# The opening of a pooling-mixer kernel: rows of both halves loaded first, stores queued behind the third product's operand, root steps on GpSimd

## The chip, the cores and the metric

The kernel runs on one core of one Trainium2 chip. Its time is the device time of one execution in microseconds (us); a kernel's time is the median over its runs. A profiled execution has its own time, and a span: from the first to the last instruction that the profiler recorded. The engines are TensorE (PE in the profile, its weight loads PEld), VectorE (DVE), ScalarE (ACT), GpSimd (POOL) and SyncE (SP), which here only issues DMAs.

## The reference

```python
def rms_norm(x, w):
    y = xf * lax.rsqrt(jnp.mean(xf * xf, axis=-1, keepdims=True) + RMS_EPS)
    return y * w

def pool_mixer(h, in_w, group_w, group_b, scale, out_w):
    u, gate = jnp.split(h @ in_w, 2, axis=-1)
    ug = u.reshape(b, s, POOL_GROUPS, POOL_GROUP_DIM)         # 4 groups of 256
    pooled = jnp.stack([trailing_mean(ug[:, :, g], w)         # windows 2, 4, 8, 16
                        for g, w in enumerate(POOL_WINDOWS)], axis=2) - ug
    mixed = jnp.einsum('bsgc,gcd->bsgd', pooled, group_w) + group_b
    y = mixed.reshape(b, s, POOL_WIDTH) * scale * jax.nn.silu(gate)
    return y @ out_w

def reference(x, norm_w, ...):                                # DEPTH = 1: mixer 0 alone
    h = x + pool_mixer(rms_norm(x, norm_w[0]), ...)
    return rms_norm(h, final_norm_w)
```

x is 1 x 4096 x 1024 (4096 rows of 1024), all in float32; in_w is 1024 x 2048, out_w 1024 x 1024, group_w four 256 x 256 matrices.

## The kernel before, in words

**Products.** Every big product is cut into 2 x 2 blocks and done by seven block products instead of eight (P1 to P7, a scheme of Strassen's kind): the operands are sums and differences of blocks, formed on VectorE, and PSUM banks gather the results. Each float32 operand is split into a high part, a copy by ScalarE (L151, `copy`), and a low part, a subtract by VectorE (L145, `sub`). `mm3` (L512) then takes three matmuls for each pair: high x high, high x low, low x high. A block product of the input side is 48 matmuls of 128 x 128 by 128 x 512: 2 halves of the depth, 4 banks, 2 parts, 3 each.

**Steps.** A list of 112 steps is written out by hand: 28 "a" steps (4 blocks of 1024 rows x seven products; the first 512 columns of gate and value), 28 "b" steps (the second 512), 56 "o" steps (8 blocks of 512 rows, out_w). Inside a block the order is `ORDER_IN = (P1, P2, P6, P7, P5, P4, P3)`, so P6 is the third product and P5 the fifth. A loop goes through the steps: it loads operands some steps ahead, forms and splits those of the next ones, runs the product's matmuls and evicts the banks. Before that loop the first two products (`run(0)`, `run(1)`) and the opening are written out by hand. A scheduler puts each engine's instructions in one in-order queue, by the order in the program, by `high_priority` and by `issue_after`, which keeps an instruction behind another one. An engine waits at the head of its queue; what stands behind waits too.

**The opening.** Fourteen dummy matmuls on a zeroed tile come first (L900). Then group_w is multiplied into the value half of in_w (`fold`, L334): two sides q = 0, 1 of four chunks; a chunk takes its part of the transposed in_w (`wut`, one 512 KB load), 16 records of a 128 x 256 matmul, and an eviction of two banks by ScalarE with the column `norm_c` (L346). The second side's four results are stored to memory (`wvd`, POOL's DMA queue, L955) and used by "b" steps. P1 of the first block follows.

**Row factors.** The rms norm's factor of each row is needed along the free axis, as P1's outputs stand with rows along it. `load_row` loads four 128-row groups for each half of a block (half 0 and 1; 512 KB each), `square_row` (L365) squares them on ScalarE with row sums into `ss`, and `stats` and `rsqrt` (L187 to L196) make 1/sqrt: mean (DVE, L372), Sqrt (ACT), reciprocal (L190) and one Newton step (four small DVE instructions of 128 x 4). In the first block `spread_rs` brings these columns to all partitions: `hl` is their split in two parts, two DVE multiplies (L389) with the identity `ident` write them out into `w[P7][0]`, and two matmuls with a tile of ones (L396) sum over partitions into bank 7, which ScalarE copies to `rstd`. Half 0 and half 1 each have such a spread, called between the banks of P1. Later blocks go through a small DRAM buffer `rd`.

**The third product's operand.** P6 of the first block needs the transposed x of both halves (tiles "11", "12", "21", "22"; loaded raw, `xt`). `normalize` (L411, by L148) multiplies "21" and "22" by rstd of half 1, `form` subtracts twice (`sub` to "21", then to "2"), `split_step(2)` splits "2" into two operand tiles `op`. `normalize_raw` does the multiplies of "11" and "12" by rstd of half 0 and stores the results (`sd`) for the "b" steps. P1's and P2's banks of the first block are evicted by DVE multiplies with rstd (`evict_in`). The weights of P7, P5, P4 and P3 are split on the way (L145 with w, `rest_of_first`), their memory being used before that for the opening's loads (`early`, `early5`).

**Tile names.** `st_…`, `vt_…`, `op_…`, `bank_…` with numbers in the prediction are uses of a tile in program order: st_91 and vt_101 hold "11" and "12" in part, vt_100 is a tile of "12", op_85 to op_88 are operand tiles in turn.

**The tail.** In the last output block sums of squares are made by halves: `early_half`, `late_factor` (one root for each of the last rows) and `late_half` (the multiply by the factor and the store).

Of the kernel before, what the change touches and what calls it, by code (L numbers as in the profile page):

```python
# [15 lines left out]
P = 128  # L16
# [44 lines left out]
def kernel(  # L61
# [82 lines left out]
    def sub(dst, a, b):  # L144
        nc.vector.tensor_tensor(out=dst, in0=a, in1=b, op=ALU.subtract)  # L145
# [7 lines left out]
    def split(dst, src):  # L153

        copy(dst[:, 0], src)
        sub(dst[:, 1], src, dst[:, 0].bitcast(F32))
# [30 lines left out]
    def rsqrt(dst, tmp, ms):  # L187

        nc.scalar.activation(tmp, ms, AF.Sqrt)
        nc.vector.reciprocal(out=dst, in_=tmp)  # L190
        mul(tmp, dst, ms)
        mul(tmp, tmp, dst)
        nc.vector.tensor_scalar(
            out=tmp, in0=tmp, scalar1=-0.5, scalar2=1.5, op0=ALU.mult, op1=ALU.add
        )
        mul(dst, dst, tmp)  # L196
# [123 lines left out]
    def load_wut(q, k, by=2):  # L320
        r = take("p (k t c) -> p k t c", early5, k=2, t=4)
        for kk in range(0, 2, by):
            nc.sync.dma_start(
                out=r[:, kk : kk + by],
                in_=wut[q, k + kk : k + kk + by].rearrange("k p t c -> p k t c"),
            )
        return r

    def fold(q, k, g, r, ps2, o, on_vector=False):

        for kk in range(2):
            for j in range(2):
                for t in range(2):
                    nc.tensor.matmul(  # L334
                        ps2[kk][:, j * 256 : (j + 1) * 256],
                        r[:, kk, 2 * j + t, :],
                        g[:, 2 * j + t, :],
                        start=(t == 0),
                        stop=(t == 1),
                    )  # L340
            if on_vector:
                last = nc.vector.tensor_scalar(
                    out=o[:, kk], in0=ps2[kk], scalar1=norm_c[k + kk], scalar2=None, op0=ALU.mult
                )
            else:
                last = nc.scalar.activation(o[:, kk], ps2[kk], AF.Copy, scale=norm_c[k + kk])  # L346
        give(r)
        return last
# [21 lines left out]
    def stats(b, half):  # L370
        ms = small.tile([P, 4], F32, tag="ms", name=f"ms{b}_{half}")
        nc.vector.tensor_scalar(  # L372
            out=ms, in0=sums[b, half], scalar1=1.0 / D, scalar2=EPS, op0=ALU.mult, op1=ALU.add
        )
        tmp = small.tile([P, 4], F32, tag="tmp", name=f"tmp{b}_{half}")
        rs = small.tile([P, 4], F32, tag="rs", name=f"rs{b}_{half}")
        rsqrt(rs, tmp, ms)
        return rs
# [3 lines left out]

    def spread_rs(half, rs):

        hl = small.tile([P, 2, 4], F32R, tag="hl", name=f"hl{half}")
        split(hl, rs)
# [8 lines left out]
        for s in range(2):  # L395
            nc.tensor.matmul(  # L396
                banks[7], ones, r[:, s, 0], start=s == 0, stop=s == 1, skip_group_check=True
            )
# [23 lines left out]

    def split_halves(us, saved=None, by_pool=False):
        ts = []
        for h, u in enumerate(us):
            t = next_op("p (s a b) -> p s a b", s=2, a=2)
            split(t, u)
            if saved is not None:
                (nc.gpsimd if by_pool else nc.scalar).dma_start(out=saved[h], in_=u)
# [30 lines left out]
    def form_in(q, b, i):  # L460
# [6 lines left out]
        elif i == P6:  # L467
            s["2"] = [take(pool=early if q == 0 and b == 0 else None) for _ in range(2)]
# [27 lines left out]

    def normalize_raw(i):

        for h, u in enumerate(xs[0]["11" if i == P1 else "12"]):
            normalize(0, 0, u)  # L500
            nc.gpsimd.dma_start(out=sd[0][i][h], in_=u)
# [6 lines left out]

    def mm3(ps, lt, r, start, stop):

        for n, (a, b) in enumerate(((lt[0], r[0]), (lt[0], r[1]), (lt[1], r[0]))):
            nc.tensor.matmul(  # L512
                ps, a, b, start=start and n == 0, stop=stop and n == 2, skip_group_check=True
            )
# [3 lines left out]
    def product_in(i, t, sets, by_bank, between=None):  # L518
# [4 lines left out]
        for n, (h, ct) in enumerate(halves):  # L523
# [3 lines left out]
            for kk in range(2):  # L527
                mm3(
                    ps[ct],
                    (w[i][h][:, 0, kk, c], w[i][h][:, 1, kk, c]),  # L530
                    (t[h][:, 0, kk], t[h][:, 1, kk]),
                    i in (P1, P7) and h == 0 and kk == 0,
                    h == 1 and kk == 1,
                )
# [174 lines left out]
    def mean_square(b, half, ss):  # L709
        n = ss.shape[1]  # L710
        ms = small.tile([P, n], F32, tag="ms", name=f"oms{b}_{half}")
        nc.vector.tensor_scalar(
            out=ms, in0=ss, scalar1=1.0 / D, scalar2=EPS, op0=ALU.mult, op1=ALU.add
        )
        return ms

    def inverse(b, half, ms):
        n = ms.shape[1]
        tmp = small.tile([P, n], F32, tag="tmp", name=f"otmp{b}_{half}")
        rs = small.tile([P, n], F32, tag="rs", name=f"ors{b}_{half}")  # L720
        rsqrt(rs, tmp, ms)
# [6 lines left out]
    def finish(b, half):  # L728
# [6 lines left out]
        rs = inverse(b, half, mean_square(b, half, ss))  # L735
# [18 lines left out]
    def mean_part(ss, before):  # L754

        ms = column()
        nc.vector.tensor_scalar(
            out=ms, in0=ss, scalar1=1.0 / D, scalar2=before, op0=ALU.mult, op1=ALU.add
        )
# [13 lines left out]
    def late_factor(half, j, parts):  # L773
# [6 lines left out]
        partial["last"] = nc.scalar.activation(tmp, ss, AF.Sqrt, bias=before, scale=1.0 / D)  # L780
        ms = mean_part(ss, before)
        nc.vector.reciprocal(out=rs, in_=tmp)
# [9 lines left out]
    def late_half(half, j, n, rs):  # L792
        rows = row_of(NBO - 1, half, j)
        u = hs[NBO - 1].pop((half, j))
        with tc.issue_after(partial["last"].ins):
            nc.scalar.activation(u[:, 1 - n], u[:, 1 - n], AF.Copy, scale=rs)
        nc.scalar.dma_start(out=out[rows, (1 - n) * H : (2 - n) * H], in_=u[:, 1 - n])
        nc.vector.scalar_tensor_tensor(
            out=u[:, n], in0=u[:, n], scalar=rs, in1=fw[0][:, n], op0=ALU.mult, op1=ALU.mult
        )  # L800
        nc.sync.dma_start(out=out[rows, n * H : (n + 1) * H], in_=u[:, n])

    def evict_o(b, i, sets):
# [5 lines left out]
        for j in range(2):  # L809
# [7 lines left out]
            for p in range(parts):  # L817
                c = slice(p * (H // parts), (p + 1) * (H // parts))
                add(u[:, c], ps[j][:, c], u[:, c])
                if last:  # L820
                    partial["part", p] = square_part(u[:, c])
            if last:
                factors.append(late_factor(half, j, parts))
        for j, rs in enumerate(factors):
# [43 lines left out]
    def run(n, between=None):  # L868
# [5 lines left out]
        else:  # L874
            product_in(i, split_up.pop(n), sets, i == P1, between)
# [23 lines left out]
    for c in range(14):  # L899
# [3 lines left out]
    nc.scalar.dma_start(out=colt, in_=cols)  # L903
# [5 lines left out]
    ru[0, 0] = load_wut(0, 0, by=1)  # L909
# [7 lines left out]
    for n, (h, k) in enumerate(chunks):  # L917
        if k < 4:
            o = v0[h] = take(pool=early)
        else:  # L920
            o = v1[h] = take()
        fold(0, k, gw[0], ru[0, k], banks[2 * (n % 2) : 2 * (n % 2) + 2], o)
        ru[1, k] = load_wut(1, k)
        if n == 0:
            load(0)
            g0.append(load_rows(in_w, 2, D))
            split_scaled(w[P1][0], g0[0], pair(norm_c, 0, 0))
        elif n == 1:
            split_step(0)
        elif n == 2:  # L930
            split_scaled(w[P1][1], g0[1], pair(norm_c, 1, 0))
        if n > 1:
            for j in range(2 * n - 4, 2 * n - 2):
                load_row(0, 0, j)
    give(gw[0])
    for j in range(4):
        load_row(0, 1, j, early if j < 1 else None)
    load(1)
    g1 = [load_rows(in_w, 4 + 2 * h, D) for h in range(2)]

# [11 lines left out]
    for n, (h, k) in enumerate(chunks):  # L952
        o = take(pool=early if n < 2 else early5)
        fold(1, k, gw[1], ru[1, k], banks[2 * (n % 2) : 2 * (n % 2) + 2], o)
        nc.gpsimd.dma_start(out=wvd[k // 2], in_=o)  # L955
        give(o)
        if n < 2:
            second_side(n)
            for j in range(2 * n, 2 * n + 2):
                square_row(0, 0, j)  # L960
            if n == 1:
                with tc.high_priority():
                    rs[0] = stats(0, 0)
        else:
            for j in range(2 * n - 4, 2 * n - 2):
                square_row(0, 1, j)
    give(gw[1])
    load(2)
# [7 lines left out]
    run(0, {1: lambda: spread(0), 5: lambda: spread(1)})  # L976
# [4 lines left out]
    normalize_raw(P1)  # L981
    for h in range(2):
        for key in ("21", "22"):
            normalize(0, 1, xs[0][key][h])
    form(2)
    split_step(2)
    run(1)
    normalize_raw(P2)
    give(rstd.pop(0))
    for h in range(2):  # L990
        split(w[P7][h], v0[h])
        give(v0[h])
# [58 lines left out]
    for n in range(2, len(steps)):  # L1051
# [22 lines left out]
        if n == 2:  # L1074
            form_s4(0)
            form(n + 2)
        if kind == "a" and b == 0:
            rest_of_first(n)
# [74 lines left out]
```

## Time and profile before

| | |
|---|---|
| median of 3 runs | 966.04 us (964.88 to 966.52) |
| profiled execution: time, span | 964.39 us, 962.6 us |
| mean granted PE clock | 0.997 |
| PE busy | 949.7 us, 99% |
| DVE busy | 748.4 us, 78% |
| ACT busy | 453.0 us, 47% |
| POOL busy | 6.7 us, 1% |
| DMA | 177.01 MB, mean 184 GB/s |

Busy time is the time in which an engine had an instruction under way; shares are of the span. A line of an answer names the source line, the engine, the operation, output<-input and the number of instructions. In the list of waits a line gives the waiting instruction, the engine and line it waited for, the total us, the number of waits and the us of one. In the chain of waits the first number is where a stretch begins (us from the start of the span) and the second how long it lasts. In the view by stretches each engine's column is the busy us of the stretch, with the number of instructions.

### The profile page before, as it was taken

How to read it: one execution, taken by the hardware profiler on the slowest of the kernel's cores; microseconds unless marked ns; L12 is line 12 of the kernel's file. 1: busy time of each engine (PE TensorE's matmuls, PEld its weight loads, DVE VectorE, ACT ScalarE, POOL GpSimd, SP SyncE). 2: the span in 40 equal slices, each digit the busy share in tenths (PEclk: the TensorE clock that was granted, in tenths of full speed). 3: DMA queues.
4: the chain of work that ended last, by engine and by line, in shares of the span. 5: the costliest groups of instructions: out<-in, count | busy, mean ns of one | idle time of the engine just before them, and what ended most of it. 6: DMA issues, size and time to landing. Idle time of an engine off the chain costs nothing.

```text
span 962.6 us, 11058 instructions
## 1 busy us (share of the span) xinstructions
PE 949.7 (99%) x4190; PEld 785.5 (82%) x4190; DVE 748.4 (78%) x919; ACT 453.0 (47%) x677; POOL 6.7 (1%) x16
## 2 busy tenths in 40 slices
PE   9999999999999999999999999999999999999996
PEld 8778888888888888888888888888888888888885
DVE  4699994893895997696697599499978667677675
ACT  5849447347445555345345445553423424324233
POOL 0110000000000000000000000000000000000000
PEclk9999999999999999999999999999999999999998
DMA  9965864564656646016614733645746436356022
GB/s 337 408 264 157 305 237 163 210 240 137 213 219 226 233 156 237 1 45 218 240 44 165 263 119 131 219 151 178 259 141 212 162 123 230 108 187 218 22 88 88
DMA packets 67685, 177.01 MB, mean 184 GB/s; under 512 B 6704, under 2 KB 24240, under 8 KB 67632
## 3 DMA queue, kind: packets, MB, share of 16 engines
q1 hardware_dynamic: 61728, 156.37, 46.8%
q10 hardware_dynamic: 4176, 13.65, 3.5%
q0 software_dynamic: 1728, 6.29, 1.6%
q8 instruction: 33, 0.54, 0.2%
q14 instruction: 20, 0.16, 0.1%
HBM read 116.50 MB, written 59.78 MB: 183 GB/s over the span
## 4 chain that ended last, share of the span: by engine, by line
PE 78%; DVE 13%; DMA 5%; ACT 3%; issue 1%; DVEq 0%; SPq 0%; ACTq 0%
PE bank L512 75%; PE bank L334 2%; DVE op L145 2%; DVE vt L142 2%; DMA st<-wvd 2%; DVE st L148 1%; DVE st L145 1%; DMA rd<-rs 1%; DVE st L598 1%; DVE w L145 1%; DMA st<-rd 1%; DVE st L261 1%; DVE vt L145 1%; DVE w L209 1%; DVE st L142 1%
## 5 line engine op out<-in xcount | busy, mean ns | idle before, releaser
L512 PE MATMUL bank<-op,w 128*128 128x512 f32 x2688 | 611.7, 389 | 2.5 <-ACT op L151 2.1
L512 PEld LDWEIGHTS bank<-op,w 128*128 128x128 f32 x2688 | 504.0, 188 | 109.1 <-ACT op L151 2.6
L512 PE MATMUL bank<-w,op 128*128 128x512 f32 (+1 forms) x1356 | 305.0, 387 | 0.0
L512 PEld LDWEIGHTS bank<-w,op 128*128 128x128 f32 x1356 | 253.0, 188 | 52.0
L151 ACT ACTIVATE op<-st 128x1024 fp32r<-128x1024 f32 x117 | 123.2, 1056 | 142.0 <-PE bank L512 112.2
L145 DVE TENSOR_TENSOR op<-st,op 128x1024 fp32r<-128x1024 f32 x117 | 141.5, 1217 | 38.7 <-ACT op L151 38.3
L151 ACT ACTIVATE op<-vt 128x1024 fp32r<-128x1024 f32 x49 | 51.8, 1059 | 92.2 <-PE bank L512 72.9
L142 DVE TENSOR_TENSOR vt<-vt 128x1024 f32<-128x1024 f32 (+6 forms) x72 | 87.7, 1227 | 0.1
L142 DVE TENSOR_TENSOR st<-bank,st 128x512 f32<-128x512 f32 x78 | 53.1, 686 | 36.9 <-PE bank L512 36.6
L145 DVE TENSOR_TENSOR op<-vt,op 128x1024 fp32r<-128x1024 f32 x49 | 59.8, 1220 | 21.7 <-ACT op L151 21.7
L151 ACT ACTIVATE vt<-bank 128x512 f32<-128x512 f32 x90 | 52.6, 595 | 46.1 <-PE bank L512 42.5
L142 DVE TENSOR_TENSOR vt<-bank,vt 128x512 f32<-128x512 f32 (+1 forms) x83 | 55.1, 677 | 15.0 <-PE bank L512 10.8
L145 DVE TENSOR_TENSOR st<-st,st 128x1024 f32<-128x1024 f32 x35 | 42.3, 1217 | 13.0 <-DMA st<-wvd 11.2
L151 ACT ACTIVATE bank<-bank 128x512 f32<-128x512 f32 x44 | 25.5, 582 | 33.9 <-PE bank L512 30.1
L145 DVE TENSOR_TENSOR w<-st,w 128x1024 fp32r<-128x1024 f32 x22 | 26.5, 1220 | 16.4 <-ACT w L151 16.2
L148 DVE TENSOR_TENSOR st<-st,st 128x1024 f32<-128x1024 f32 (+1 forms) x18 | 20.4, 1160 | 19.6 <-DMA st<-rd 18.3
L151 ACT ACTIVATE w<-st 128x1024 fp32r<-128x1024 f32 x22 | 23.1, 1059 | 22.9 <-PE bank L512 15.4
L151 ACT ACTIVATE st<-bank 128x512 f32<-128x512 f32 x36 | 21.2, 596 | 21.1 <-PE bank L512 19.1
L593 DVE SCALAR_TENSOR_TENSOR vt<-vt,vt 128x1024 f32<-128x1024 f32 x24 | 29.2, 1217 | 0.1
L334 PE MATMUL bank<-early,early 128*128 128x256 f32 x128 | 27.8, 379 | 0.0
L334 PEld LDWEIGHTS bank<-early,early 128*128 128x128 f32 x128 | 24.3, 190 | 3.3
L598 DVE SCALAR_TENSOR_TENSOR st<-vt,colt,st 128x512 f32<-128x512 f32 x36 | 25.6, 742 | 0.0
(116 smaller groups left out, 449.7 us busy)
## 6 DMA issues: line engine op xcount, KB each, us to landing
st<-in_x SPq DMA_DIRECT2D x34, 512.0 KB, 4.5
vt<-in_x SPq DMA_DIRECT2D x25, 512.0 KB, 4.5
st<-sd SPq DMA_DIRECT2D x25, 512.0 KB, 5.4
st<-in_xt SPq DMA_DIRECT2D x24, 512.0 KB, 6.1
sd<-st ACTq DMA_DIRECT2D x19, 512.0 KB, 6.4
st<-yd SPq DMA_DIRECT2D x19, 512.0 KB, 3.7
yd<-st SPq DMA_DIRECT2D x18, 512.0 KB, 2.9
out<-st SPq DMA_DIRECT2D x17, 512.0 KB, 4.8
```

The costliest lines, as they stand in the source:

```text
L142: nc.vector.tensor_tensor(out=dst, in0=a, in1=b, op=ALU.add)
L145: nc.vector.tensor_tensor(out=dst, in0=a, in1=b, op=ALU.subtract)
L148: nc.vector.tensor_tensor(out=dst, in0=a, in1=b, op=ALU.mult)
L151: return nc.scalar.activation(dst, src, func)
L209: nc.vector.scalar_tensor_tensor(out=dst[:, 1], in0=u, scalar=c, in1=dst[:, 0].bitcast(F32), op0=ALU.mult, op1=ALU.subtract,)
L261: nc.vector.scalar_tensor_tensor(out=u[:, j], in0=u[:, j], scalar=cs[j], in1=other[:, j], op0=ALU.mult, op1=op)
L334: nc.tensor.matmul(ps2[kk][:, j * 256 : (j + 1) * 256], r[:, kk, 2 * j + t, :], g[:, 2 * j + t, :], start=(t == 0), stop=(t == 1),)
L512: nc.tensor.matmul(ps, a, b, start=start and n == 0, stop=stop and n == 2, skip_group_check=True)
L593: nc.vector.scalar_tensor_tensor(out=s[:, :, at : at + H], in0=s[:, :, at : at + H], scalar=1.0 / win, in1=v[:, :, HIST:], op0=ALU.mult, o ...
L598: nc.vector.scalar_tensor_tensor(out=sg[:, j], in0=s[:, j, at : at + H], scalar=bias_c[2 * grp + j], in1=sg[:, j], op0=ALU.add, op1=ALU.mult,)
```

## The change

It does the following.

- **Dummies and first loads.** Eight dummies instead of fourteen. The first half of the first wut chunk is issued by ScalarE's queue, ahead of the columns' load.
- **Rows.** The four rows of half 0 are all loaded behind the second chunk of the first side, those of half 1 with more of the early memory; `load(2)` moves up. Squares of half 0 go ahead of `second_side`; all four of half 1 come behind the folds.
- **Folds.** One of the two banks of each chunk of the second side is evicted by VectorE.
- **Roots.** `rsqrt` takes mean and eps into ScalarE's Sqrt; the mean and the Newton step (four instructions after the reciprocal) go to GpSimd, for the opening, for later blocks and for the output blocks. The low part of `hl` goes to GpSimd as well.
- **Spreads.** The second spread is called behind P1's last bank and its matmuls are kept behind the last matmul issued; P2 goes bank by bank, and its second group is kept behind the spread.
- **Third product's operand.** Its normalizes, subtracts and splits are written out half by half ahead of P2's run; the multiplies of "12", the low parts of P7's weights and `rest_of_first` stand behind the last low split (`latest_split`).
- **Stores.** The wvd stores and those of `normalize_raw` are gathered in `stores` and issued at step 2 on GpSimd, behind the first save of that step.
- **Tail.** In the last block the multiply of one row (`late_half`) is held back until the next product's first row has its factor, and VectorE's multiplies of `late_half` stay behind the last add.

```diff
     def sub(dst, a, b):
-        nc.vector.tensor_tensor(out=dst, in0=a, in1=b, op=ALU.subtract)
+        return nc.vector.tensor_tensor(out=dst, in0=a, in1=b, op=ALU.subtract)
...
-        sub(dst[:, 1], src, dst[:, 0].bitcast(F32))
+        latest_split[0] = sub(dst[:, 1], src, dst[:, 0].bitcast(F32)).ins
...
-    def rsqrt(dst, tmp, ms):
-        nc.scalar.activation(tmp, ms, AF.Sqrt)
+    def rsqrt(dst, tmp, ms, ss):
+        nc.scalar.activation(tmp, ss, AF.Sqrt, bias=eps, scale=1.0 / D)
+        nc.gpsimd.tensor_scalar(
+            out=ms, in0=ss, scalar1=1.0 / D, scalar2=EPS, op0=ALU.mult, op1=ALU.add
+        )
         nc.vector.reciprocal(out=dst, in_=tmp)
-        mul(tmp, dst, ms)
-        mul(tmp, tmp, dst)
-        nc.vector.tensor_scalar(
+        nc.gpsimd.tensor_tensor(out=tmp, in0=dst, in1=ms, op=ALU.mult)
+        nc.gpsimd.tensor_tensor(out=tmp, in0=tmp, in1=dst, op=ALU.mult)
+        nc.gpsimd.tensor_scalar(
             out=tmp, in0=tmp, scalar1=-0.5, scalar2=1.5, op0=ALU.mult, op1=ALU.add
         )
-        mul(dst, dst, tmp)
+        nc.gpsimd.tensor_tensor(out=dst, in0=dst, in1=tmp, op=ALU.mult)
...
-    def fold(q, k, g, r, ps2, o, on_vector=False):
+    def fold(q, k, g, r, ps2, pool=None, on_vector=()):
...
-            if on_vector:
-                last = nc.vector.tensor_scalar(
+            if kk in on_vector:
+                nc.vector.tensor_scalar(
...
-        split(hl, rs)
+        copy(hl[:, 0], rs)
+        nc.gpsimd.tensor_tensor(
+            out=hl[:, 1], in0=rs, in1=hl[:, 0].bitcast(F32), op=ALU.subtract
+        )
...
+        with tc.issue_after(latest[0]):
+            for s in range(2):
+                spread_done[0] = nc.tensor.matmul(
+                    banks[7], ones, r[:, s, 0], start=s == 0, stop=s == 1, skip_group_check=True
+                ).ins
...
-            nc.gpsimd.dma_start(out=sd[0][i][h], in_=u)
+            stores.append((sd[0][i][h], u))
...
+            with tc.issue_after(behind) if behind and n == 1 else nullcontext():
...
+        if between and 8 in between:
+            between[8]()
...
-        nc.vector.scalar_tensor_tensor(
-            out=u[:, n], in0=u[:, n], scalar=rs, in1=fw[0][:, n], op0=ALU.mult, op1=ALU.mult
-        )
+        with tc.issue_after(partial["added"]):
+            nc.vector.scalar_tensor_tensor(
+                out=u[:, n], in0=u[:, n], scalar=rs, in1=fw[0][:, n], op0=ALU.mult, op1=ALU.mult
+            )
...
+                if i == P3 and j == 0:
+                    late_half(*partial.pop("waiting"))
+        if final and i == P4:
+            partial["waiting"] = (half, 1, n, factors.pop())
...
-    for c in range(14):
+    for c in range(8):
...
-    ru[0, 0] = load_wut(0, 0, by=1)
+    ru[0, 0] = load_wut(0, 0, (nc.scalar, nc.sync))
+    nc.scalar.dma_start(out=colt, in_=cols)
...
         elif n == 1:
+            ru[1, 4] = load_wut(1, 4)
+            for j in range(4):
+                load_row(0, 0, j)
             split_step(0)
-        elif n == 2:
-            split_scaled(w[P1][1], g0[1], pair(norm_c, 1, 0))
-        if n > 1:
-            for j in range(2 * n - 4, 2 * n - 2):
-                load_row(0, 0, j)
+        else:
+            ru[1, k] = load_wut(1, k)
+            if n == 2:
+                split_scaled(w[P1][1], g0[1], pair(norm_c, 1, 0))
     give(gw[0])
     for j in range(4):
-        load_row(0, 1, j, early if j < 1 else None)
+        load_row(0, 1, j, early if j < 3 else None)
...
-        o = take(pool=early if n < 2 else early5)
-        fold(1, k, gw[1], ru[1, k], banks[2 * (n % 2) : 2 * (n % 2) + 2], o)
-        nc.gpsimd.dma_start(out=wvd[k // 2], in_=o)
-        give(o)
+        o = fold(1, k, gw[1], ru[1, k], banks[2 * (n % 2) : 2 * (n % 2) + 2], early5, (0,))
+        stores.append((wvd[k // 2], o))
         if n < 2:
-            second_side(n)
             for j in range(2 * n, 2 * n + 2):
                 square_row(0, 0, j)
...
+            second_side(n)
...
-    run(0, {1: lambda: spread(0), 5: lambda: spread(1)})
+    run(0, {1: lambda: spread(0), 8: lambda: spread(1)})
...
     normalize_raw(P1)
+    s = xs[0]
+    s["2"] = [take(pool=early) for _ in range(2)]
+    split_up[2] = []
     for h in range(2):
         for key in ("21", "22"):
-            normalize(0, 1, xs[0][key][h])
-    form(2)
-    split_step(2)
-    run(1)
-    normalize_raw(P2)
-    give(rstd.pop(0))
+            normalize(0, 1, s[key][h])
+        sub(s["21"][h], s["11"][h], s["21"][h])
+        sub(s["2"][h], s["22"][h], s["21"][h])
+        split_up[2] += split_halves([s["2"][h]])
     for h in range(2):
-        split(w[P7][h], v0[h])
-        give(v0[h])
+        copy(w[P7][h][:, 0], v0[h])
+    run(1, behind=spread_done[0])
+    with tc.issue_after(latest_split[0]):
+        normalize_raw(P2)
+        give(rstd.pop(0))
+        for h in range(2):
+            sub(w[P7][h][:, 1], v0[h], w[P7][h][:, 0].bitcast(F32))
+            give(v0[h])
...
         if n == 2:
+            with tc.issue_after(first_saves[0]):
+                for place, u in stores:
+                    nc.gpsimd.dma_start(out=place, in_=u)
...
             form_s4(0)
             form(n + 2)
         if kind == "a" and b == 0:
-            rest_of_first(n)
+            with tc.issue_after(latest_split[0]):
+                rest_of_first(n)
```

## The prediction

> **What bounds it now.** I read the waits of TensorE (PE) first, then the chain of waits, then the busy time by stretches, then the timelines of VectorE (DVE) and GpSimd (POOL) in the opening. The waits of PE are short:
>
> ```profile
> PE bank L512 <- ACT op L151: 2.1, 1, 2.1
> PE bank L900 <- DVE op L898: 1.5, 1, 1.5
> PE bank L396 <- DVE w L389: 1.2, 1, 1.2
> PE bank L512 <- DVE op L145: 0.4, 2, 0.2
> ```
>
> PE waits 5.2 us in 962.6. From 66 us on its matmuls start 226.7 ns apart, so nothing after the opening can be won but the two 0.2 us waits (at 127.1 and 367.0 us) and the tail. The 2.1 us stand before the third product (P6), at 60.88; the 1.2 us before the L396 matmuls, at 36.80.
>
> ```profile
> 127.32 98.01 PE bank L512 x431
> ...
> 367.17 587.77 PE bank L512 x2603
> 954.96 0.44 DVE vt L142
> ```
>
> The chain of waits runs through DVE from 97.83 to 127.32 and from 258.74 to 367.17 and through PE between: PE is caught by DVE at just these places. The stretches say why:
>
> ```profile
> 3.00:4.00 1.00, 1.00 (x4) 0.81 (x3) 0.00 (x0) 0.30 (x2) 0.00 (x0) 1.00 1.08 376
> 5.00:6.00 1.00, 1.00 (x6) 0.80 (x5) 0.00 (x0) 0.00 (x0) 0.00 (x0) 1.00 1.02 352
> 15.00:25.00 10.00, 10.00 (x48) 8.79 (x48) 8.41 (x10) 8.29 (x12) 0.13 (x1) 1.00 1.03 400
> 62.00:72.00 10.00, 9.98 (x45) 8.02 (x44) 10.00 (x12) 5.00 (x6) 0.53 (x1) 1.00 0.17 66
> 72.00:82.00 10.00, 10.00 (x46) 8.28 (x45) 10.00 (x12) 9.38 (x14) 0.00 (x0) 1.00 0.19 54
> ```
>
> Columns: busy PE, weight load, DVE, ACT, POOL, then PE clock, DMA share, GB/s. The DMA engines are full (share 1.0) from 3 us to 60 us; DVE is full (10.00 of 10) from 48 to 85 us. And its queue there ends just in time:
>
> ```profile
> 81.39 1.22 DVE L145 TENSOR_TENSOR w<-early,w 128x1024 fp32r<-128x1024 f32 x1
> 82.52 0.16 DVE L372 TENSOR_SCALAR ms<-ss 128x4 f32<-128x4 f32 x1
> 82.60 2.35 DVE L145 TENSOR_TENSOR op<-st,op 128x1024 fp32r<-128x1024 f32 x2
> 85.09 0.18 DVE L190 RECIPROCAL rs<-tmp 128x4 f32<-128x4 f32 x1
> ```
>
> The 82.60 line makes the low halves of the operand of the fifth product, P5 (the first ready at 83.81). P5 starts 96 matmuls after P6: 61.19 (60.88 with its waits taken in) + 96 x 0.2267 = 82.95; its four high-half matmuls take it to 83.86, when it needs that operand. Spare: 0.05 us.
>
> **Dummies and the first loads.** The x14 dummies take 427 ns apart until 5.03 us and 230 after (the x3 and x6 of the stretches). Eight end at 1.45 + 0.60 + 7 x 0.427 = 5.03, so the folds (L334, 0.2155 us each, 16 to a chunk, 3.45 us) may start at 5.03 instead of 6.41: -1.4 us. The first wut half goes by ACT's queue at 0.73; with one group half it is 512 KB, which the trace of before moved by 4.65 us. But the DMA engines are full, 1.30 us for 512 KB, and four rows of x now go ahead of the last two wut chunks: the chunk that landed at 22.48 comes fifth after the one of 21.14, at 21.14 + 5 x 1.30 = 27.6. The seventh chunk could start at 5.03 + 6 x 3.45 = 25.7: PE waits 2 us there, P1 can start at 27.7 + 6.9 = 34.55 (before: 33.84). The 1.4 us are gone.
>
> **First root.** The half-0 rows land at 22.4 to 26.3 (before 23.8 to 29.1). ACT in its new order, from the eviction at 25.95: 0.65, square 1.14, weight copy 1.05, square 1.14, table load 1.28, Sqrt 0.2: 31.3. Then one reciprocal (0.18), four POOL steps of p each, ACT's hl copy 0.2, a POOL subtract, two DVE L389-type steps (0.61, 0.65) and, behind these in DVE's queue, an eviction (0.66) for which P1's first matmul waits: P1 starts at 33.85 + 4p, or 34.55 if that is later. The 1.2 us wait inside P1 goes, since the spread is made before P1.
>
> p: no row shows arithmetic on POOL. Below it lies a POOL memset, above it a DMA issue:
>
> ```profile
> 0.35 0.10 POOL L1138 MEMSET const-uint8-127<- 128x1 uint8 x1
> 24.87 0.67 POOL L955 DMA_DIRECT2D wvd<-early  x1 [24.43 <-ACT early L346]
> 28.32 0.53 POOL L955 DMA_DIRECT2D wvd<-early  x1 [2.78 <-ACT early L346]
> ```
>
> So 0.10 to 0.53; I take 0.25, since the same dependent column steps on DVE stand 0.20 to 0.25 apart (948.52, 948.72, 948.97, 949.16). P1: 34.85. The Trainium skill (GPSIMD Engine Reference, section 3.1) measures a two-input elementwise step at 1.96 times DVE's; by it p would be 0.4 (an estimate from DVE's 0.20), and the sum below would end at -0.6 us instead of -1.5.
>
> **Second root and third product.** Behind hl (32.85) ACT has: square 1.14, eviction 0.65, two squares 2.2, eviction 0.65, square 1.14, rstd copy 0.6, Sqrt 0.2: 39.2. DVE: a multiply (1.2), reciprocal 40.4, POOL 4p to 41.45, hl 41.7; DVE by then has an eviction and a split to do, and starts the second spread at T0 = 42.1 (p = 0.25; 41.5 at 0.10, 44.1 at 0.53). Before: 47.57. That is the gain of the row order: 5.5 us. From T0 to P6's first low operand DVE has 11 x 1.13 (multiplies, subtracts, splits), 6 x 0.61 and 3 x 0.66: 17.1 us with the last one's full time, so 59.2, and P6's start with its waits taken in is 59.2 - 2 x 0.227 = 58.75, against 61.19: -2.4 us. P2 ends at 34.85 + 100 x 0.227 + 0.3 = 57.8, so about 0.9 us of wait is left. The eight stores queue on POOL behind the P7 save; 8 x 0.53 of issue and 8 x 1.30 of transfer from 53 us, over before DVE's subtract from the stored tiles at 70: no wait. If that cover is gone, DVE's in-order queue stops there, with P5's operand behind it (a rival).
>
> **Where most of it goes back.** DVE's work is not less, only in another order. In before, second spread to P5's first low operand is 83.81 - 47.57 = 36.24 us with no gap. Now stand behind T0, ahead of before: two evictions (2 x 0.61), the split of op_88, the multiplies of st_91 and vt_100 (3 x 1.13) and one weight step (0.66): 5.27; one small step (0.08) goes. T0 + 41.5 = 83.6. P5 then starts at 83.65 - 0.91 = 82.75, against 82.95: **-0.2 us**, though PE could come there at 58.75 + 21.76 = 80.5. PE stands about 2 us before P5 instead of before P6.
>
> **After that.** Between 84.95 and 127.26 DVE idles 2.9 us in before and spends 0.9 us on ten small root steps, which go to POOL; its products' operands then come 3 us ahead. The wait at 127 and the matmul steps beside it (0.085 + 0.34 + 0.11) go: -0.5. At 367 the chain holds roots whose steps stand between big ones (246.28 to 252.56, 6.3 us); on POOL they take 1 us, so 0.35 + 0.11 go: -0.5. Tail: the last root's DVE steps no longer wait for the multiply of the other row at the same place: reciprocal at 956.95 instead of 957.25: -0.3. The root steps of the output blocks are beside the matmuls and cost nothing; their cover is the PE bound. **Sum: -0.2 - 0.5 - 0.5 - 0.3 = -1.5 us**, from the profiled execution's 964.39 (span 962.6 and 1.8 around it) to 962.9; the median of the runs lies 1.65 above that execution, so 966.04 - 1.5 = 964.5. A measurement tells about 0.2% (1.9 us) from no change, so the forecast is "no change" by a little.
>
> **Rivals.**
> *The third product's gain is kept.* If POOL steps cost a memset's 0.10 and ACT's and DVE's queues run a little tighter than I add up, T0 is 41.5 or less: -2.2 at 41.5; with T0 at 39.5 PE never waits at P5 and all of 2.4 + 1.3 = 3.7 us is won. For it: full queues whose starts I add with 0.05 to 0.1 us each. Against: the 36.24 us without a gap.
> *Slow POOL steps* (the slower side). T0 moves by about 8p once p is over 0.25, as both roots go through POOL and ACT waits for each. At 0.53 T0 is 44.1, P5 is 1.75 late, sum +0.5; at 1 us T0 is 47.8 and the sum +4.2. It decides from p = 0.47. For: nothing shows POOL computing. Against: its four memsets start 0.04 us apart. A slow first step is the same mechanism. The Trainium skill (GPSIMD Engine Reference, section 2.1, Instruction dispatch) states some 6 us for the first call of freshly loaded code; by it POOL's first step, behind the ss of 29.8, would end at 35.8, and the sum would be about +2.6 us (an estimate); no run here shows it.
> *The stores.* Eleven saves go through POOL's queue in one order, and DVE's subtract from vt_100 (behind it all of P5's operand) waits for the tenth. If each takes POOL 1.3 us rather than 0.53, or lands after 7 us as the first wvd stores did (24.87 to 32.85 by the trace), DVE stops 2 to 4 us: sum +1 to +2.5.
> *Nothing moves*: the late places find new waits of the same size; 0 +- 0.5.
>
> **Chances.** Forecast 0.45 (its own range -2.6 to -0.4: a third of it over 0.2% faster); gain kept 0.28; slow POOL 0.15 (0.05 of it within 0.2%); stores 0.10, slower; nothing moves 0.02. Faster 0.16 + 0.28 = 0.44, same 0.29 + 0.05 + 0.02 = 0.36, slower 0.10 + 0.10 = 0.20. Range: from the kept gain (966.04 - 3.7 = 962.3) to the dear end of the stores (966.04 + 2.5 = 968.5), which takes in p of 0.53 (+0.5) on the way; left out is p beyond 0.75.
>
> **What would show it.** PE waits: about 2 us before the seventh fold chunk (25.7 to 27.7), none at the spread, under 1 us at P6, about 2 us at P5 on a DVE op; none at 127 and 367. First P1 matmul near 34.8, second spread's DVE step near 42.1, POOL's root steps near 0.25 us apart. Wrong if P5 starts without a wait, if POOL's steps are 0.5 us or more apart, or if DVE waits for a store near 70 us.

## The result, and the profile after

The kernel after takes 974.01 us (median of 6 runs, 972.36 to 978.58) against 966.28 for the kernel before on the same chip: ratio 1.0083, 95% interval 1.0063 to 1.0103. It is slower by 0.8%, where 964.5 was forecast. Its profiled execution took 972.92 us with a span of 971.1, 8.5 more than the 962.6 of before. The profiled execution of before took 1.9 us less than its median and that of after 1.1 less, so 8.5 us in the profiles stand for 7.7 in the medians.

The waits of TensorE after:

```profile
PE bank L534 <- DVE op L145: 7.0, 6, 2.8
PE bank L344 <- DMA early<-in_wut: 2.4, 1, 2.4
PE bank L927 <- DVE op L925: 1.5, 1, 1.5
```

The waits at the spread and on ScalarE are gone; there is a new one in the folds and 7.0 us, in six places, on low halves that VectorE makes. The chain of waits has its two long PE stretches 4.6 and 7.5 us later than before (127.32 and 367.17):

```profile
131.96 98.09 PE bank L534 x431
...
374.64 589.38 PE bank L534 x2603
```

The busy time by stretches (PE, weight load, DVE, ACT, POOL, then PE clock, DMA share, GB/s) shows something that before has not:

```profile
30.00:34.00 4.00, 4.00 (x12) 3.20 (x11) 1.05 (x3) 2.48 (x6) 1.17 (x6) 0.57 1.03 410
371.00:375.00 4.00, 1.69 (x8) 1.07 (x8) 4.00 (x5) 3.79 (x6) 0.00 (x0) 1.00 0.42 159
375.00:379.00 4.00, 4.00 (x12) 3.18 (x11) 4.00 (x4) 0.68 (x1) 0.00 (x0) 0.57 0.61 235
```

In 30 to 34 us and 375 to 379 us the granted clock is 0.57 and PE gets through 12 matmuls where before it took 21 and 19: after the waits of 2.36 us (26.67 to 29.03) and 2.31 us (372.33 to 374.64), eight matmuls in a row ran at that clock, some 427 ns apart. That is 1.7 us more for the first wait (8 x 0.213) and 1.6 for the second (8 x 0.200).

P5's operand, whose end was forecast near 83.6 us, is the first of the pair at 85.37, done at 86.59:

```profile
84.15 1.22 DVE L145 TENSOR_TENSOR w<-early,w 128x1024 fp32r<-128x1024 f32 x1
85.28 0.17 DVE L198 RECIPROCAL rs<-tmp 128x4 f32<-128x4 f32 x1
85.37 2.33 DVE L145 TENSOR_TENSOR op<-st,op 128x1024 fp32r<-128x1024 f32 x2
```

The lag of TensorE against before, the same matmul taken in both profiles: P1's first 37.51 against 33.84 (+3.7); P6's, behind its waits, -0.3; P5's fifth, the first that needs the low operand, 86.62 against 83.99 (+2.6, and +2.7 from the next on); 131.96 against 127.32 (+4.6); 374.64 against 367.17 (+7.5); the last matmul's end 964.00 against 954.92 (+9.1, with the half clock behind 374.64); the span +8.5, as the tail is 0.55 shorter. From 379 to 950 us the lag does not move. So 2.7 us go in the opening, where the forecast had a gain of 0.2, and 6.4 in the loop, where it had a gain of 1.0. Below, P5's time is that of its fifth matmul.

### The profile page after: what moved, and what is told of

The parts are those of the page before. It is cut to its first block, busy times and chain, and to the rows that moved or that the text cites. A ratio compares the mean times of both kernels' runs of the same rounds, so it can differ in the third digit from the quotient of the medians.

```text
span 971.1 us, 11098 instructions
## 1 busy us (share of the span) xinstructions
PE 953.2 (98%) x4184; PEld 787.4 (81%) x4184; DVE 738.3 (76%) x811; ACT 450.8 (46%) x673; POOL 48.4 (5%) x129
## 4 chain that ended last, share of the span: by engine, by line
PE 72%; DVE 14%; DMA 9%; issue 2%; ACT 2%; POOL 0%; SPq 0%; ACTq 0%; DVEq 0%; POOLq 0%
PE bank L534 71%; DVE op L145 2%; DMA st<-wvd 2%; DVE vt L142 2%; DVE vt L148 1%; DVE st L148 1%; DMA early<-in_wut 1%; DVE st L623 1%; DVE st L145 1%; DMA vt<-in_in_w 1%; DVE vt L145 1%; DVE st L142 1%; DVE w L217 1%; DMA rd<-rs 1%; DMA st<-in_xt 1%
## 5 line engine op out<-in xcount | busy, mean ns | idle before, releaser
L151 ACT ACTIVATE op<-st 128x1024 fp32r<-128x1024 f32 x113 | 119.3, 1056 | 146.0 <-PE bank L534 139.2
L145 DVE TENSOR_TENSOR op<-st,op 128x1024 fp32r<-128x1024 f32 x113 | 137.7, 1222 | 59.2 <-ACT op L151 58.7
L151 ACT ACTIVATE op<-vt 128x1024 fp32r<-128x1024 f32 x53 | 55.9, 1058 | 85.0 <-PE bank L534 81.0
L142 DVE TENSOR_TENSOR vt<-vt 128x1024 f32<-128x1024 f32 (+6 forms) x72 | 88.0, 1232 | 0.2
L145 DVE TENSOR_TENSOR op<-vt,op 128x1024 fp32r<-128x1024 f32 x53 | 64.5, 1221 | 13.2 <-ACT op L151 13.2
L840 DVE TENSOR_TENSOR st<-bank,st 128x512 f32<-128x512 f32 x60 | 41.3, 689 | 40.5 <-PE bank L534 40.4
L145 DVE TENSOR_TENSOR st<-st,st 128x1024 f32<-128x1024 f32 x34 | 41.3, 1223 | 14.4 <-DMA st<-wvd 13.8
L148 DVE TENSOR_TENSOR st<-st,st 128x1024 f32<-128x1024 f32 (+1 forms) x20 | 22.9, 1167 | 25.0 <-DMA st<-rd 21.6
L195 POOL TENSOR_SCALAR oms<-oss 128x2 f32<-128x2 f32 x14 | 8.6, 611 | 643.0 <-ACT st L751 638.5
L145 DVE TENSOR_TENSOR w<-st,w 128x1024 fp32r<-128x1024 f32 x22 | 26.5, 1222 | 15.0 <-ACT w L151 14.8
L840 DVE TENSOR_TENSOR vt<-bank,vt 128x512 f32<-128x512 f32 (+1 forms) x37 | 24.9, 674 | 16.4 <-PE bank L534 16.4
L344 PE MATMUL bank<-early,early 128*128 128x256 f32 x128 | 30.5, 402 | 2.4 <-DMA early<-in_wut 2.4
L142 DVE TENSOR_TENSOR vt<-bank,vt 128x512 f32<-128x512 f32 x46 | 30.6, 684 | 0.2
```

The costliest lines, as they stand in the source:

```text
L142: nc.vector.tensor_tensor(out=dst, in0=a, in1=b, op=ALU.add)
L145: return nc.vector.tensor_tensor(out=dst, in0=a, in1=b, op=ALU.subtract)
L148: nc.vector.tensor_tensor(out=dst, in0=a, in1=b, op=ALU.mult)
L151: return nc.scalar.activation(dst, src, func)
L195: nc.gpsimd.tensor_scalar(out=ms, in0=ss, scalar1=1.0 / D, scalar2=EPS, op0=ALU.mult, op1=ALU.add)
L344: nc.tensor.matmul(ps2[kk][:, j * 256 : (j + 1) * 256], r[:, kk, 2 * j + t, :], g[:, 2 * j + t, :], start=(t == 0), stop=(t == 1),)
```

## The experiments

Ratios are to the kernel before in the same runs, with 95% intervals. Three theories were put up: A, the late first product; B (E further on), the price of GpSimd's steps themselves; C, the order of VectorE's queue behind the second spread. D, added later, is the order of VectorE's queue in the later blocks. Blocks are counted from 0.

**Fillers in the fold's wait.**

```diff
+        if n == 2:
+            for c in range(10):
+                nc.tensor.matmul(banks[4 + c % 4], warm[:, 0:P], warm, ...)
         o = fold(1, k, gw[1], ...)
```

> The kernel after, with ten dummy matmuls of 0.21 us put on TensorE ahead of the seventh chunk of folds, where it waited 2.36 us (26.69 to 29.03) for its wut; eight matmul pairs then ran at half the granted clock (30.4 to 33.8), 1.7 us. Theory A (late first product): the late wut and the half clock make P1 3.7 us late (37.51 against 33.84); the first spread's matmuls stand behind P1's first bank, DVE idles 3.45 us at 36.93 waiting for them, and P5's operand comes late. By A: no half clock, P1 near 35.8, DVE's idle near 1.8, P5 1 to 1.7 us earlier, the time 1 to 1.7 us under the kernel after (near 972.5). Theory B (GpSimd's root steps, 1.05 us each where a DVE instruction with two SBUF inputs was first) and theory C (what stands in DVE's queue between the second spread and P5's operand, 42.6 us against 36.2): P1 earlier, P5 and the time unchanged within 0.5 us.

978.95 us, 1.0107 (1.0074 to 1.0139): not faster than the change. The profiled execution took 972.89 us, while four of the six runs took 978 to 981; what made those slow stands in no profile. In the profile the half clock behind the fold went, but the wut came 1 us later, so P1 started at 36.81, P5 at 86.22 (only 0.4 earlier); and now twelve matmuls behind P5's 2.83 us wait ran at half clock (86.81 to 91.93), 2.4 us. The half clock had only found another wait, and this run doesn't settle A.

**Two rows behind the seventh wut.**

```diff
             ru[1, 4] = load_wut(1, 4)
-            for j in range(4):
+            for j in range(2):
                 load_row(0, 0, j)
...
             if n == 2:
+                for j in range(2, 4):
+                    load_row(0, 0, j)
```

> The kernel after, with two of the four rows of half 0 loaded behind the seventh chunk's wut instead of ahead of it. By A: that wut lands two transfers (2.6 to 4 us) earlier, near 24.9, no wait before the seventh chunk, at most 0.5 before the eighth, no half clock, P1 near 34, DVE's idle before rstd under 1.5, the wait before P5 from 2.77 to under 1, the time 3 to 4 us under the kernel after (970 to 971). By B and C: P1 earlier by 3.5, but P5's wait over 2 us and the time within 1 us of the kernel after.

970.19 us, 1.0036 (1.0021 to 1.0050): 3.8 under the kernel after, 4.1 if each is taken against the kernel before in its own runs; A had 3 to 4. No wait in the folds; VectorE stood 0.56 us instead of 3.45 ahead of its first multiply with rstd; P5 started at 83.14, 3.5 earlier, though still after a wait of 1.98 (A had under 1). But at 372 this execution was as late as the kernel after: 374.97 against 374.64. The loop loses on its own.

**Fold evictions on ScalarE.**

```diff
-        o = fold(1, k, gw[1], ru[1, k], banks[...], early5, (0,))
+        o = fold(1, k, gw[1], ru[1, k], banks[...], early5)
```

> The kernel after, with all evictions of the second side's folds on ScalarE, as before (DVE loses four instructions of 0.75 us). If DVE's amount of work up to P5's operand is what counts, P5 comes up to 3 us earlier and the time falls by up to 3; if DVE only waits longer for rstd at 36.93 (theory A: the idle time grows by what the work shrinks, and ScalarE's squares come later), P5 and the time stay within 1 us.

973.45 us, 1.0087 (1.0060 to 1.0115): nothing won. P1 started at 34.43, 3.1 earlier, and P5 at 87.08, 0.5 later. The timeline of VectorE says why:

```profile
33.83 1.48 DVE L403 TENSOR_TENSOR w<-early,hl 128x512 fp32r<-128x512 f32 x2 [1.46 <-DMA vt<-in_xt]
40.78 1.23 DVE L148 TENSOR_TENSOR st<-st,st 128x1024 f32<-128x1024 f32 x1 [5.47 <-ACT st L151]
```

The multiply at 40.78 stood 5.47 us for ScalarE's copy of the row factor (the bracket), against 3.45 after. That copy, not P1 as such, starts VectorE's unbroken stretch to P5.

**All root steps on VectorE.**

```diff
-        nc.gpsimd.tensor_scalar(out=ms, in0=ss, ...)
+        nc.vector.tensor_scalar(out=ms, in0=ss, ...)
 ... (the four Newton steps and the low part of hl likewise)
```

> The kernel after, with all root steps that went to GpSimd (means, Newton steps, the low part of the spread's columns) back on VectorE. Theory B: GpSimd's blocked steps (1.0 to 1.3 us instead of 0.2) are the loss: the second spread starts 1 us earlier or more, the waits at 118 to 131 us and at 372 go, the time falls by 3 to 5 us. Theories A and C: the seventh chunk's wait and the half clock stay, P1 at 37.5, P5's wait stays over 2 us; the time changes by less than 1.5 us either way.

966.64 us, 0.9999 (0.9990 to 1.0009): the whole loss gone with this edit alone, more than the 3 to 5 us that B had, though P5 still waited 3.13 us. Its second spread began at 43.94, against 44.00, where B had 1 us earlier or more. But P1 came at 34.54 in this profile, 3.0 earlier, so the opening is not the same; the next run parts the opening from the later blocks.

**GpSimd's roots in the opening alone; and on the kernel before alone.**

```diff
+        rsqrt(rs, tmp, ms, sums[b, half], nc.gpsimd if b == 0 else nc.vector)
```

> The kernel after, with GpSimd's root steps kept for the first block alone; the means and Newton steps of the later blocks and of the output blocks are back on VectorE. With all roots on VectorE the kernel after went from 974.0 to 966.6. If the loss is in the later blocks (a GpSimd step behind a running DVE instruction took 1.05 us instead of 0.19, and DVE's queue waits for the row factor that comes of it): the waits at 118 to 131 and at 372 us shrink to those of the kernel before, P5's wait (2.8) stays, time 969.5 to 971. If it is in the opening (VectorE's queue and the second spread wait for GpSimd there): time within 1 us of 974.

> The kernel before, with only the root steps moved to GpSimd as in the change (and mean and eps taken into ScalarE's Sqrt). If these steps alone carry the loss: 4 to 8 us slower than before (970 to 974), with a wait before P5 of 2 us or more and one near 370. If they only do harm together with the new order of the opening: within 1.5 us of before.

967.21 us, 1.0008 (0.9993 to 1.0022), under the 969.5 to 971 expected, and 976.07 us, 1.0093 (1.0073 to 1.0113), over the 970 to 974 expected. With GpSimd's roots in the opening alone the second spread began at 43.42. The loss is in the roots of the later blocks, and the root steps alone make the kernel before as slow as the whole change (there with a wait of 4.1 us before P6, as the opening's queue changes too, and one of 2.5 at 375).

Is it GpSimd's own time? Its timeline, for the opening's first root and for block 1's second:

```profile
32.45 0.20 POOL L199 TENSOR_TENSOR tmp<-rs,ms 128x4 f32<-128x4 f32 x1 [1.75 <-DVE rs L198]
32.73 0.20 POOL L200 TENSOR_TENSOR tmp<-tmp,rs 128x4 f32<-128x4 f32 x1
33.02 0.19 POOL L201 TENSOR_SCALAR tmp<-tmp 128x4 f32<-128x4 f32 x1
...
102.42 1.03 POOL L199 TENSOR_TENSOR tmp<-rs,ms 128x4 f32<-128x4 f32 x1 [0.41 <-DVE rs L198]
103.53 0.20 POOL L200 TENSOR_TENSOR tmp<-tmp,rs 128x4 f32<-128x4 f32 x1
103.82 0.19 POOL L201 TENSOR_SCALAR tmp<-tmp 128x4 f32<-128x4 f32 x1
104.10 1.09 POOL L204 TENSOR_TENSOR rs<-rs,tmp 128x4 f32<-128x4 f32 x1
```

Of 112 steps in the kernel after 89 took 0.19 us and 23 took 1.05 on the mean, all of these under a VectorE instruction with two inputs in SBUF (at 102.42 the L148 of 102.19). That is dearer than forecast, but the loss has another place. VectorE in block 3, after:

```profile
251.33 0.17 DVE L198 RECIPROCAL rs<-tmp 128x4 f32<-128x4 f32 x1
...
256.19 1.22 DVE L142 TENSOR_TENSOR vt<-vt 128x1024 f32<-128x1024 f32 x1
262.42 1.23 DVE L148 TENSOR_TENSOR st<-st,st 128x1024 f32<-128x1024 f32 x1 [5.01 <-DMA st<-rd]
263.56 1.22 DVE L618 SCALAR_TENSOR_TENSOR vt<-vt,vt 128x1024 f32<-128x1024 f32 x1
264.70 1.22 DVE L145 TENSOR_TENSOR op<-st,op 128x1024 fp32r<-128x1024 f32 x1
265.83 0.68 DVE L142 TENSOR_TENSOR st<-bank,st 128x512 f32<-128x512 f32 x1
```

and before:

```profile
246.28 0.16 DVE L190 RECIPROCAL rs<-tmp 128x4 f32<-128x4 f32 x1
...
252.53 1.23 DVE L593 SCALAR_TENSOR_TENSOR vt<-vt,vt 128x1024 f32<-128x1024 f32 x1
253.67 1.22 DVE L145 TENSOR_TENSOR op<-st,op 128x1024 fp32r<-128x1024 f32 x1
254.81 1.28 DVE L142 TENSOR_TENSOR st<-bank,st 128x512 f32<-128x512 f32 x2
258.74 1.23 DVE L148 TENSOR_TENSOR st<-st,st 128x1024 f32<-128x1024 f32 x1 [2.65 <-DMA st<-rd]
```

The L148 at 262.42 (258.74 before) needs the row factor, which goes through DRAM. From the reciprocal to it took 11.1 us after and 12.5 before, so GpSimd's root is not slower. But the scheduler put L148 four instructions sooner: L618, L145 and two L142, 3.5 us of ready work, now stand behind it, and VectorE idles 5.01 us instead of 2.65. In block 1 the reciprocal itself moved ahead of an eviction of P5 and stood 5.79 us (96.31 to 102.09). VectorE is behind from there, and TensorE catches up with it at 118 to 131 and at 349 to 372.

**The order pinned, roots left on GpSimd.** If so, holding only those places must bring the time back.

```diff
-                    scales[j // 4] = stats(b + 1, j // 4)
+                    with tc.issue_after(added[P5]) if j > 3 and b == 0 else nullcontext():
+                        scales[j // 4] = stats(b + 1, j // 4)
...
-            normalize_a2(b)
+            with tc.issue_after(added[P4]):      # P4's second eviction
+                normalize_a2(b)
```

> The kernel after with all root steps still on GpSimd, and two places of VectorE's queue held as in the kernel before: the reciprocal of block 1's half 1 behind the third product pair's last eviction (P5's), and the normalizes of half 1 of the later blocks behind P4's second eviction. In the profile after, VectorE stood 5.8 us at that reciprocal (96.3) and 5.0 us at that normalize (257.4), with ready work queued behind; with the later roots on VectorE it stood 2.9 and 2.4. Theory D (order): the loss of the later blocks is this order alone; the standing falls to 3 and 2.5 us, the waits of TensorE at 118 to 131 and 372 us to under 0.7 each, the time to 967 to 970. Theory E (blocked steps): GpSimd's steps at 1.05 us are the price themselves; the time stays at 973 to 975.

967.38 us, 1.0008 (0.9995 to 1.0021), as D said. The blocked steps are still there (24 of 1.04 us). VectorE's standing in block 3, now behind that work:

```profile
257.12 1.22 DVE L145 TENSOR_TENSOR op<-st,op 128x1024 fp32r<-128x1024 f32 x1
258.25 1.28 DVE L142 TENSOR_TENSOR st<-bank,st 128x512 f32<-128x512 f32 x2
261.37 1.22 DVE L148 TENSOR_TENSOR st<-st,st 128x1024 f32<-128x1024 f32 x1 [1.84 <-DMA st<-rd]
```

In block 1 it is 2.90 instead of 5.79. TensorE's waits of 0.3 us and more are gone between 87 and 400 us.

**Each place alone.**

> The kernel after, with only the normalizes of half 1 of the later blocks held behind P4's second eviction. If the last late place sets the time (the wait at 372 came to +7.5 to 8 us against before in every kernel with this order, whatever the lag before it): the wait at 372 falls to what the earlier lag leaves, the waits at 118 to 131 stay, the time falls by 4 to 6 us, to 968 to 970. If both places add up: by about 2 to 4.

> The kernel after, with only the reciprocal of block 1's half 1 held behind P5's last eviction. If the last late place sets the time: the waits at 118 to 131 shrink to under 0.5 in all, but the wait at 372 grows by as much, and the time stays within 1 us of the kernel after (973 to 975). If both places add up: 1.5 to 3 us under it.

968.71 us, 1.0043 (1.0025 to 1.0060), and 969.22 us, 1.0037 (1.0021 to 1.0052). Taken against the kernel before in the same runs, the normalize alone won 4.8 of the 7.7 us lost, within the 4 to 6 expected, and the reciprocal alone 4.3, where at most 1 was expected if the last late place sets the time: that idea fell. Both together won 7.7. That is less than the sum of 9.1, but by no more than the intervals allow, so whether the two places add is not shown.

Both medians hide two groups of runs: seven at 967.3 to 969.0 and five at 971.8 to 974.2 with the normalize held, eight at 967.5 to 970.2 and four at 972.2 to 973.7 with the reciprocal held. The profiled execution of the latter took 973.0 us, and in it one GpSimd step was held far longer than any other:

```profile
85.08 8.95 POOL L199 TENSOR_TENSOR tmp<-rs,ms 128x4 f32<-128x4 f32 x1 [7.40 <-ACT w L151]
91.62 2.34 DVE L145 TENSOR_TENSOR w<-st,w 128x1024 fp32r<-128x1024 f32 x2
93.89 0.67 DVE L142 TENSOR_TENSOR vt<-bank,vt 128x512 f32<-128x512 f32 x1
```

It ended at 94.03, behind eight L145 in a row (84.83 to 93.96); in the kernel after the same step took 0.99. The L148 that needs its factor then stood 5.14 us, to 102.23 (97.23 with both places held), and TensorE waited 0.62, 1.75, 0.80 and 0.39 us between 109 and 136, where under 0.5 in all was expected. So a held step can cost time by itself (E), in some executions. Whether such a step makes the slower groups is not shown: each kernel has one profile.

**Both losses repaired.** Four kernels: all roots on VectorE and rows two and two; the same with the fold evictions on ScalarE; the same with the order of before behind the second spread; and rows two and two with GpSimd's roots pinned. Their edits are those above; the third undoes this:

```diff
-    run(1, behind=spread_done[0])
-    with tc.issue_after(latest_split[0]):
-        normalize_raw(P2)
-        ...
+    split_step(2)          # after the normalizes, then the subtracts of both halves
+    run(1, behind=spread_done[0])
+    normalize_raw(P2)
...
-            with tc.issue_after(latest_split[0]):
-                rest_of_first(n)
+            rest_of_first(n)
```

> The kernel after with two edits undone: all root steps on VectorE, and two rows of half 0 loaded behind the seventh chunk's wut. Alone the first took 7.4 us off the kernel after, the second 3.8. If the two losses are separate, the sum is 962.8, 0.4% faster than before, with P5's wait under 1 us and no half clock. If both act through the same place (DVE's queue between the first spread and P5's operand), the second adds little: 965 to 966.6.

966.08 us, 0.9990 (0.9979 to 1.0002): the two repairs don't add. Each taken against the kernel before in its own runs, they won 7.7 and 4.1 us alone and 8.0 together. P1's first matmul came at 30.65, P5 at 84.64 after a wait of 3.65.

> The kernel with all roots on VectorE and rows two and two (966.08; P5 started at 84.64 against 82.95 before), and the evictions of the second side's folds all on ScalarE. If VectorE's amount of work ahead of P5's operand (four evictions of 0.75 us) is what is left: P5 1.5 to 3 us earlier, 963 to 964.6. If ScalarE, which makes the row factor's copies in the same queue, comes late instead (as in the first run with these evictions on ScalarE, where VectorE stood 5.5 us and nothing was won): 966 to 967.5.

967.26 us, 1.0002 (0.9991 to 1.0013): the second case, P5 at 85.17.

> The kernel with all roots on VectorE and rows two and two, and the order of the kernel before behind the second spread (no instruction held behind the third product's last split). By the listed order VectorE has 37.6 us from the second spread to P5's first operand instead of 38.8, and 17.1 us instead of 14.2 to P6's. If the order behind the spread is worth what it takes: P6 waits 2 to 3 us more, P5 1 us less in all, the time within 1 us of 966.1; if that order was the gain, 2 us slower (968).

965.83 us, 0.9989 (0.9978 to 0.9999), within 1 us: P6 waited 2.14 us, P5 not at all. The wait only changes its place; that order was no gain and no loss.

> As the one before, and two rows of half 0 loaded behind the seventh chunk's wut (alone 3.8 us under the kernel after). By D and a separate loss in the opening: 964 to 967, within 0.2% of the kernel before with all roots on GpSimd. By E: 969 to 971.

965.70 us against 967.35 for the kernel before in the same runs, 0.9981 (0.9967 to 0.9996): the lowest ratio of all, under both kernels, though 0.9989 and 0.9990 above lie within its interval. In the profile TensorE is 0.7 us behind before from 400 us on (span 962.8), and the shorter tail gives it back; the profile of before is of an execution faster than most.

**The tail alone.**

> The kernel before, with only the change of the last output block (late_half of one row held back). In the profile after, the last matmul's end to the end of the span took 7.1 us, before 7.68. Expected by all theories: that stretch 7.1 to 7.4, the time 0.3 to 0.6 us less, all else the same.

965.56 us, 0.9992 (0.9978 to 1.0007): not told from no change by the time. In its profile the stretch from the last matmul's end is 7.23 us, against 7.68.

## Why the prediction was wrong

- *What bounds it*: right. P5's operand had 0.05 us to spare, VectorE was full to 85 us, and the loss came at the places named (P5, 127, 367).
- *Dummies and first loads*: mechanism right, size off. The seventh chunk's wut landed at 28.90 (27.6 forecast), as five transfers took 7.9 us and not 6.5; the wait was 2.36 (2). Missing in the sum was the half clock behind it, 1.7. P1 at 37.51, not 34.85.
- *First root*: right but for 0.8 us (Sqrt done at 32.1, forecast 31.3). The steps started 0.28 us apart (0.25). Not foreseen: 0.70 for the low part of hl under L403.
- *Second root*: T0 was 44.00, not 42.1. P1's first matmuls stood ahead of the spread's, so P1's delay went on into rstd, and VectorE stood 3.45 us at 36.93. One GpSimd step of this root was held (42.40, 1.05).
- *Third product*: P6's first low operand was done at 61.28 (59.2), T0's delay; of the gain of 2.4, 0.3 came.
- *Where most of it goes back*: T0 to that operand's end was 42.6 us (41.5), of which 0.76 is a wait for a store (that rival had 2 to 4). With T0's delay the operand was 3.0 late; P5 came 2.7 late against before, where 0.2 early was forecast.
- *After that*: this is the step that failed. It took the root steps off VectorE's queue and left the rest in its order, -0.5 and -0.5. The order was the scheduler's to make anew, and it put the instructions that wait for the root sooner: +6.4 instead of -1.0, of which 1.6 is the half clock. The forecast worked from the new order in the opening alone; VectorE's new queue between each later reciprocal and the instruction that needs its factor would have told it.
- *Tail*: -0.55 in the profile (-0.3).
- *Rivals*: slower came true, but not by its mechanism. Slow POOL steps decide from p = 0.47, and 89 of 112 steps took 0.19; in the opening GpSimd cost nothing that the runs tell (967.21 us with its roots there, 966.64 without). Of the 6 us that the prediction gave a first step nothing is seen: the first one took 0.19 at 30.51. Nor does its factor of 1.96 hold for steps of 128x4: 0.19 against VectorE's 0.15 to 0.17. (By the prediction's own values of T0, p = 0.4 would have given a sum near -0.4, not -0.6.)

## What to carry to other kernels

When small dependent steps move to another engine, the in-order queue that they leave is scheduled anew: look in the built order at what now stands behind each instruction that waits for their result, for that was the price in the kernel after; the steps' own time was seen to cost in one execution of another kernel. Taking 3.5 us of ready work back ahead of one kind of wait won 4.8 of the 7.7 us lost. And repairs of a queue that is late in several places need not add: two were worth 7.7 and 4.1 us alone and 8.0 together.

## What the runs showed of the hardware

**A wait of 2 us can cost more than itself.** In the profiles of all the kernels here TensorE waited between 1.97 and 4.08 us 22 times; behind 16 of these waits it then ran 4 to 13 matmuls at 427 ns instead of 227, 0.8 to 2.6 us more. Behind the 25 waits of 0.90 to 1.88 us none ran slow; the wait of 1.5 us at the very start, behind which every kernel's dummies run slow, is left out. In the kernel after the 2.36 and 2.31 us waits were followed by such a stretch, the 2.77 us one was not. The two stretches lie 344.9 us apart (33.76 to 378.62), 101 times 3.415. And in the records of the granted clock of all 16 profiles, each of the 48 changes after a profile's first lies a whole number of 3.4133 us from that first one, within 0.02 us. The Trainium skill (TensorE: Matmul & The Clock Gate, Part 1) tells of a free-running window of 3413 ns that sets the clock; the trace agrees with the window. The page names one idle window of about 3.4 us as the condition for the slower clock; here a wait of 1.97 us was enough, so the measurement decides.

What counts is how much of a wait falls into one window. With the windows laid by the clock's records, between the opening and the last matmul, TensorE idled 1.95 to 3.41 us in 16 windows at full clock, and each of them was followed by one at half clock; in all other windows at full clock it idled at most 1.75 us, and none of them was. The 2.36 us wait put 1.99 us into one window (27.04 to 30.45). The 2.77 us wait was cut in two, 1.22 and 1.55 us (81.65 to 85.07 to 88.48), and went unpunished. No run moved a wait inside its window on purpose.

**GpSimd stands still under VectorE.** In the kernel after a step took 1.05 us instead of 0.19 in 23 of 112 cases, each beside a VectorE instruction with two SBUF inputs. Beside an eviction, with one input in PSUM, a step was not held up (103.53 beside the eviction of 103.32: 0.20). The Trainium skill (SBUF — State Buffer, SBUF: two separate sides) states this: the pair of ports that the two engines share is locked for a whole instruction, and the other one blocks. The trace agrees. A step can also be kept out through several instructions: in the profile of the kernel with the reciprocal alone held, one took 8.95 us under eight L145 in a row.
